# RWKV-7 inside a two-layer trunk: head sums in column blocks of the array, a group norm spread over three steps, and state products pinned next to each other

## The chip, the core and the metric

The kernel runs on one core of a Trainium2 chip. A core has a matrix engine (TensorE, "PE" in the profile, with its weight loads as "PEld"), a vector engine (VectorE, "DVE"), an engine for activations and copies (ScalarE, "ACT"), a general engine (GpSimd, "POOL"), and a sync engine ("SP") that issues most transfers. Each engine works through its own queue in order; they wait for each other through semaphores. The metric is the time of one execution on the device in microseconds (us), the median of several runs.

## The reference

The program is one decoder trunk of two layers on 512 tokens of width 1024, in float32: layer 0 mixes tokens with an RG-LRU block, layer 1 with RWKV-7; each is followed by a gated feed-forward block with a width of 3072. The change touches layer 1's mixer alone:

```python
def _rwkv7_scan(r, w, k, v, aa, bb):
    def step(S, inp):
        r_t, w_t, k_t, v_t, a_t, b_t = inp
        sa = jnp.einsum('bhij,bhj->bhi', S, a_t)
        S = S * w_t[:, :, None, :] + sa[..., None] * b_t[:, :, None, :] + v_t[..., :, None] * k_t[..., None, :]
        y = jnp.einsum('bhij,bhj->bhi', S, r_t)
        return S, y
    ...

def _rwkv7_block(x, ...):
    ...
    r, k, v = rkv[0], rkv[1], rkv[2]
    w = -jax.nn.softplus(-(w0 + jnp.tanh(xw @ w1) @ w2).astype(f32)) - 0.5
    decay = jnp.exp(-jnp.exp(w))
    a = jax.nn.sigmoid((a0 + (xa @ a1) @ a2).astype(f32))
    g = jax.nn.sigmoid(xg @ g1) @ g2
    kk = (kf * k_k).reshape(bsz, seq, RWKV_H, RWKV_N)
    kk = kk / jnp.maximum(jnp.linalg.norm(kk, axis=-1, keepdims=True), 1e-12)
    kf = kf * (1.0 + (a - 1.0) * k_a)
    ...
    y = _rwkv7_scan(rh, hs(decay), kh, vh, -kk, kk * ah)
    mu = jnp.mean(y, axis=-1, keepdims=True)
    var = jnp.mean(jnp.square(y - mu), axis=-1, keepdims=True)
    y = ((y - mu) * lax.rsqrt(var + GN_EPS)).reshape(bsz, seq, d) * ln_w + ln_b
    bonus = jnp.sum(rh * kh * r_k, axis=-1, keepdims=True) * vh
    y = (y + bonus.reshape(bsz, seq, d)).astype(x.dtype)
    return jnp.einsum('btd,de->bte', y * g, w_out)
```

There are 16 heads of 64 channels. Two sums run over the 64 channels of each head: the norm of `kk`, and the bonus. The group norm is over the 64 channels of a head as well.

## The kernel before

**Layout.** Activations lie with channels on the 128 partitions (8 blocks of 128 channels, two heads each) and the 512 tokens along the free dimension. The exact products against large weights are made of three fp32r products, high by high, high by low and low by high (`mm3`, lines 47 to 53); these are the `acc` rows of the profile. Small products with plain float32 operands are recorded as two matmul instructions each. PSUM has 8 banks of 128 x 512 floats, all taken from one pool (`bank`, line 77).

**Who sets the order.** The program is written as a foreground (the large projections) and background tasks, generators that are advanced by a counted number of units between the foreground's products (`push`, `background`, lines 55 to 65; three lanes). From this text a planner makes the order of each engine's queue: it takes what its own timing model believes to be ready, by the order in the text where several are. `tc.keep_in_program_order(ins)` pins an instruction behind the one that the text has just before it on the same engine.

**The decay and the gate `a`** (`second`, inside `rwkv_lora_k`, lines 819 to 851). For each of the 8 blocks two products are made, `l2w` and `l2a`, each a 128-row product followed by a 64-row one into the same bank (lines 840 and 841, 848 and 849). The 64-row product of `l2w` reads partitions 0 to 63, that of `l2a` 64 to 127. They run in the background of the key projection.

**The norm of the keys** (`prepare`, lines 900 to 952). For each half H of the heads (4 blocks) a square `sq` is computed per block and summed over each head by a product with `sel`, a matrix of 8 columns with ones, accumulated over the four blocks into 8 rows of bank `ssq` (line 915). The 8 rows are copied, transposed to tokens (`sst`, line 930), and inverted. It runs behind the key and receptance projections.

**The bonus** (`bonus`, lines 1286 to 1303) has the same form: product `pr` on VectorE, sum over the head by `selk` (8 columns that hold r_k, line 1294) into bank `bon`, copy, transpose (`bont`, line 1300), copy to `bons[H]`.

**The chunk steps** (`rwkv_chunks`, from line 1082). The 512 tokens are 8 chunks of 64. Step n (0 to 16) advances two groups of 4 heads, the second one step behind the first; H=0 takes steps 0 to 8, H=1 steps 8 to 16. A step (`step`, lines 1187 to 1248) issues on TensorE:

- `pe` (line 1200), 8 small products on the state `sv`, copied to `e1`
- the next step's products `s` (`prep_s`), masked by VectorE into `W`
- `between()`, which advances a tail of the group norm, then `fill(0)`: background units
- `pu` and the first part of `py` (lines 1213, 1216), copied to `uv` (line 1220); `prep_t` (transposes `tr`); `fill(1)`
- `pd` (line 1229), from which VectorE makes the next state (lines 1237, 1238, 1240), then the second part of `py` (line 1243), copied to `ytok` (line 1247); `fill(2)`

All heads of a step share one order: for each product the two groups alternate, and the two groups write different column halves of the array.

**The group norm** (`tail`, lines 1250 to 1279), once for every two steps, has three parts. Part one: mean, difference, square (ACT), variance, and a power on POOL (line 1266); also `bv`, the bonus times v, on POOL (line 1263). Part two: three VectorE products (lines 1269 to 1271), the first pinned. Part three: four transposes `pz` on TensorE and four ACT copies into the array that the output projection reads. Part one is issued at the end of an even step, part two in the middle of the next one (`between`), part three at that next step's end.

**The end.** From step 10 the fills are units of `first_half`: four gate products for blocks 0 to 3, then the first half of the output projection (16 units of 6 products). After step 16 come four gate products for H=1, 5.9 units, parts two and three of the last tail, 1.1 units, and the rest (lines 1399 to 1407), then the second half of the output projection. The tag `sq` (three buffers of 128 x 512) is shared by `pr`, `bt`, `ysq`, `bv` and the gate product `yg`.

## Time and profile before

| what | us |
|---|---|
| median of 3 runs (lowest, highest) | 1350.35 (1349.07, 1352.65) |
| the profiled execution | 1353.01 |
| its span, first to last instruction | 1351.3 |

In the profiled execution the layer's stages lie about here: decay, gate and keys 588 to 700 us, the solve of the chunks' triangular systems for H=0 up to 744, steps 0 to 8 from 744 to 838, steps 9 to 16 to 907, the end of the output's first half to 921. A granted clock of 1.00 is TensorE's full speed.

How to read the rows below. A row of the timeline is: start, duration, engine, line, operation, output and inputs, shape, count; in brackets the idle time of the engine before it and what ended it. TensorE's products overlap in their shown durations, so that the distance between two starts is what a product takes. A row of windows is: stretch and its length, then busy time and number of instructions of PE, PEld, DVE, ACT and POOL, the granted clock, the share of the DMA engines, GB/s.

### The profile page before, as it was taken

The numbers are of one execution on the slowest core, as the hardware profiler recorded it, in microseconds if no ns is written. First come the engines' busy times: TensorE is split into PE (matmuls) and PEld (weight loads), VectorE is DVE, ScalarE is ACT, GpSimd is POOL, SyncE is SP. The second block draws the span as 40 slices with busy tenths as digits, with TensorE's granted clock in tenths as the row PEclk, the third lists the DMA queues.
The fourth block names the chain that finished last, engine by engine and source line by source line (L and its number), as shares of the span: only waits on it lengthen the run. The fifth ranks groups of instructions, "written<-read, shape, count | busy, mean of one in ns | idle before, by whom it ended". The sixth has DMA issues, their size and how long they took to land.

```text
span 1351.3 us, 20246 instructions
## 1 busy us (share of the span) xinstructions
PE 1315.4 (97%) x8339; PEld 1062.6 (79%) x8339; DVE 865.4 (64%) x1332; ACT 613.8 (45%) x968; POOL 67.8 (5%) x110
## 2 busy tenths in 40 slices
PE   8999999999999999999999988898999999999998
PEld 7877888888888888866769776676888888888886
DVE  5988756555445756497897977776646464365623
ACT  6797534233233423378635457554634242244311
POOL 4000000000000000020011011120000000000000
PEclk8999999999999999999999889898999999999999
DMA  5423333222323433122222111122323232333311
GB/s 182 121 63 94 100 103 104 84 92 66 108 92 108 128 112 127 56 79 79 63 61 74 56 36 65 56 64 63 113 90 106 66 94 80 109 97 130 115 63 63
DMA packets 72124, 120.27 MB, mean 89 GB/s; under 512 B 9498, under 2 KB 21476, under 8 KB 71904
## 3 DMA queue, kind: packets, MB, share of 16 engines
q1 hardware_dynamic: 70672, 117.20, 27.9%
q8 instruction: 65, 1.06, 0.3%
q10 hardware_dynamic: 576, 1.05, 0.2%
q0 software_dynamic: 784, 0.74, 0.2%
q14 instruction: 27, 0.22, 0.1%
HBM read 114.44 MB, written 4.52 MB: 88 GB/s over the span
## 4 chain that ended last, share of the span: by engine, by line
PE 89%; DVE 5%; ACT 3%; issue 1%; POOL 1%; DMA 1%; SPq 0%; POOLq 0%; ACTq 0%; DVEq 0%
PE acc L51 22%; PE acc L52 22%; PE acc L53 22%; PE acc L616 3%; PE acc L615 3%; PE acc L617 3%; PE acc L986 1%; PE s L1157 1%; PE acc L987 1%; PE acc L988 1%; PE pe L1200 1%; PE ssq L915 1%; PE pd L1229 1%; POOL mu L1266 1%; DMA xin<-in_x_dram 1%
## 5 line engine op out<-in xcount | busy, mean ns | idle before, releaser
L51 PE MATMUL acc<-xs,wh 128*128 128x512 f32 x896 | 352.1, 393 | 0.0
L52 PE MATMUL acc<-xs,wh 128*128 128x512 f32 x896 | 349.9, 390 | 0.0
L53 PE MATMUL acc<-xs,wl 128*128 128x512 f32 x896 | 349.1, 391 | 0.7 <-DVE wl L91 0.7
L91 DVE TENSOR_TENSOR wl<-raw,wh 128x1024 fp32r<-128x1024 f32 (+1 forms) x201 | 242.8, 1216 | 166.3 <-PE acc L52 92.4
L90 ACT CAST wh<-raw 128x1024 fp32r<-128x1024 f32 (+1 forms) x201 | 208.1, 1045 | 259.9 <-DVE wl L91 165.8
L53 PEld LDWEIGHTS acc<-xs,wl 128*128 128x128 f32 x896 | 168.6, 188 | 36.8 <-DVE wl L91 1.2
L51 PEld LDWEIGHTS acc<-xs,wh 128*128 128x128 f32 x896 | 168.8, 188 | 34.8 <-ACT wh L90 0.2
L52 PEld LDWEIGHTS acc<-xs,wh 128*128 128x128 f32 x896 | 168.8, 188 | 34.6 <-issue 0.2
L576 DVE SCALAR_TENSOR_TENSOR cv<-gpad,pv,cv 128x512 f32<-128x512 f32 x96 | 71.9, 749 | 22.2 <-ACT cv L574 21.1
L90 ACT CAST hid<-un 128x512 fp32r<-128x512 f32 x48 | 29.8, 620 | 108.6 <-DVE un L583 108.6
L616 PE MATMUL acc<-wh,hid 128*128 128x512 f32 (+1 forms) x200 | 76.8, 384 | 0.0
L615 PE MATMUL acc<-wh,hid 128*128 128x512 f32 (+1 forms) x200 | 76.5, 383 | 0.0
L617 PE MATMUL acc<-wl,hid 128*128 128x512 f32 (+1 forms) x200 | 75.9, 380 | 0.0
L52 PE MATMUL acc<-hid,wh 128*128 128x512 f32 x192 | 75.7, 394 | 0.0
L53 PE MATMUL acc<-hid,wl 128*128 128x512 f32 x192 | 75.6, 394 | 0.0
L51 PE MATMUL acc<-hid,wh 128*128 128x512 f32 x192 | 75.5, 393 | 0.0
L582 DVE TENSOR_TENSOR un<-acc,rb 128x512 f32<-128x512 f32 x48 | 33.0, 688 | 44.3 <-PE acc L53 44.3
L91 DVE TENSOR_TENSOR hid<-un,hid 128x512 fp32r<-128x512 f32 x48 | 33.2, 691 | 31.4 <-ACT hid L90 31.4
L574 ACT ACTIVATE cv<-gpad,pv 128x512 f32<-128x512 f32 x48 | 39.2, 817 | 20.3 <-DVE gpad L571 20.1
L578 ACT ACTIVATE ge<-cv 128x512 f32<-128x512 f32 x48 | 30.1, 627 | 35.9 <-DVE cv L576 35.9
L620 DVE TENSOR_TENSOR xtok<-xtok,acc 128x512 f32<-128x512 f32 (+1 forms) x25 | 16.7, 666 | 45.2 <-PE acc L617 45.2
L615 PEld LDWEIGHTS acc<-wh,hid 128*128 128x128 f32 x200 | 37.5, 188 | 8.0
(425 smaller groups left out, 2211.9 us busy)
## 6 DMA issues: line engine op xcount, KB each, us to landing
raw<-in_ffn_w_up_dram SPq DMA_DIRECT2D x96, 512.0 KB, 3.9
raw<-in_ffn_w_down_dram SPq DMA_DIRECT2D x48, 512.0 KB, 3.7
raw<-in_rwkv_w_rkv_dram SPq DMA_DIRECT2D x24, 512.0 KB, 3.8
raw<-in_lru_w_in_dram SPq DMA_DIRECT2D x16, 512.0 KB, 3.9
raw<-in_lru_w_out_dram SPq DMA_DIRECT2D x8, 512.0 KB, 3.7
raw<-in_rwkv_w_out_dram SPq DMA_DIRECT2D x8, 512.0 KB, 3.5
xd<-x SPq DMA_DIRECT2D x8, 256.0 KB, 2.0
AR<-xd SPq DMA_DIRECT2D x1, 2048.0 KB, 9.1
```

Of the source, the lines that this page charges most:

```text
L51: nc.tensor.matmul(ps, wh, xh, start=start, stop=False)
L52: nc.tensor.matmul(ps, wh, xl, start=False, stop=False)
L53: nc.tensor.matmul(ps, wl, xh, start=False, stop=stop)
L90: (self.nc.vector.tensor_copy if dve else self.nc.scalar.copy)(hi, src)
L91: self.nc.vector.tensor_tensor(lo, src, hi.bitcast(F32), ALU.subtract)
L574: nc.scalar.activation(cv, gp[:, 0:T], AF.Identity, bias=self.vec(f"ffn_conv_b{l}", fb), scale=cw(0))
L576: nc.vector.scalar_tensor_tensor(cv, gp[:, j : j + T], cw(j), cv, ALU.mult, ALU.add)
L578: nc.scalar.activation(ges[o], cv, AF.Gelu_apprx_tanh)
L582: nc.vector.tensor_tensor(un, ps, rbs[0], ALU.mult)
L615: nc.tensor.matmul(ps, hh[:, s], wh[:, k, m], start=kk == 0, stop=False)
L616: nc.tensor.matmul(ps, hl[:, s], wh[:, k, m], start=False, stop=False)
L617: nc.tensor.matmul(ps, hh[:, s], wl[:, k, m], start=False, stop=kk == 7)
```

## The change

1. **Decay and gate.** Both products of a block get their banks at once: the two 128-row products first, a unit later the two 64-row products next to each other, with row positions 0 and 64.
2. **Head sums.** The sums of `prepare` and `bonus` no longer accumulate over four blocks in 8 rows. Block j writes its own 32 rows of the bank, from a weight of 32 columns at column position 32 j, and the sums are issued in pairs, after the second, and after the fourth block. The copy and the four transposes take all 128 rows; the two useful rows of each 32 are picked out behind them.
3. **Order of the state products.** `pe`, `pd` and the second part of `py` take the two groups in reverse order, and each product is pinned behind the one before it.
4. **Group norm.** `between()` moves from the middle of a step to its end, behind the state's update and `py`; a tail's part two is then issued at the end of the step after part one, part three at the end of the step after that. In step 9 it is called in the middle too, so that both parts run in that step. The first transpose of part three is pinned.
5. **Fills.** Lane 2 gets 1.3, 1.8, 2.0 units per step instead of 1.4, 2.0, 2.1 in the first eight steps; lane 1 gets 0.8 and 1.3 instead of 0.9 and 1.6 from step 8 on. After step 16 part two of the last tail comes first, then the gate products, 3 units, part three, 1 unit.

```diff
@@ second
-                ps = self.bank("l2w")
-                nc.tensor.matmul(ps, ws[0][0][:, s], tw, start=True, stop=False)
-                nc.tensor.matmul(ps, ws[0][1][0:64, s], tw[0:64, :], start=False, stop=True)
+                pw, pa = self.bank("l2w"), self.bank("l2a")
+                nc.tensor.matmul(pw, ws[0][0][:, s], tw, start=True, stop=False)
+                nc.tensor.matmul(pa, ws[1][0][:, s], ta, start=True, stop=False)
+                yield 1
+
+                nc.tensor.matmul(pw, ws[0][1][0:64, s], tw[0:64, :], start=False, stop=True, tile_position=(0, 0))
+                nc.tensor.matmul(pa, ws[1][1][64:128, s], ta[64:128, :], start=False, stop=True, tile_position=(64, 0))
...
@@ prepare
-                nc.tensor.matmul(ssq[0:8, :], sel[:, j, 0:8], sq, start=j == 0, stop=j == 3)
+                sqs.append(sq)
+                for i in (j - 1, j) if j % 2 else ():
+                    nc.tensor.matmul(ssq[32 * i : 32 * i + 32, :], sel[:, 0, 0:32], sqs[i], start=True, stop=True, tile_position=(0, 32 * i))
...
-            ss = t("tmp", 2)[0:8]
-            nc.scalar.copy(ss, ssq[0:8])
+            ss = t("tmp", 2)
+            nc.scalar.copy(ss, ssq)
...
-                nc.tensor.transpose(pt[:, c * 8 : c * 8 + 8], ss[:, c * P : (c + 1) * P], self.ident[0:8, 0:8])
+                nc.tensor.transpose(pt[:, c * P : (c + 1) * P], ss[:, c * P : (c + 1) * P], self.ident)
...
@@ step
+            late = [(i, h, G) for i in range(2) for h in range(2) for G in gs[::-1]]
+            chained = lambda first, ins: ins if first else tc.keep_in_program_order(ins)
...
-            for i, h, (g, bs, H, c, c2, q) in heads:
+            for n_, (i, h, (g, bs, H, c, c2, q)) in enumerate(late):
                 bh = half(1 - q)
-                nc.tensor.matmul(pe[bh, i, h], W[:, h, 2 * g + i, bh], sv[:, 2 * g + i, h], start=True, stop=True, tile_position=(0, 64 - q * 64))
+                chained(n_ == 0, nc.tensor.matmul(pe[bh, i, h], W[:, h, 2 * g + i, bh], sv[:, 2 * g + i, h], start=True, stop=True,
+                                                  tile_position=(0, 64 - q * 64)))
...
-            between()
+            if n == NC + 1:
+
+                between()
             fill(0)
...
+            between()
             fill(2)
@@ tail
-                nc.tensor.transpose(pz[:, i * P : (i + 1) * P], ytok[H, c2][:, i, :], self.ident)
+                put = tc.keep_in_program_order if i == 0 else lambda ins: ins
+                put(nc.tensor.transpose(pz[:, i * P : (i + 1) * P], ytok[H, c2][:, i, :], self.ident))
...
@@ bonus
+                prs.append(pr)
                 yield 1
-                nc.tensor.matmul(pn[0:8, :], selk[:, b, :], pr, start=i == 0, stop=i == 3)
+
+                for j in (i - 1, i) if i % 2 else ():
+                    nc.tensor.matmul(pn[32 * j : 32 * j + 32, :], selk[:, H * 4 + j, :], prs[j], start=True, stop=True, tile_position=(0, 32 * j))
...
@@ the steps' loop
-        self.fills = ((1.2, 1.1, 0.2), (1.0, 0.9, 1.9), (1.4, 2.0, 2.1))
+        self.fills = ((1.2, 1.1, 0.2), (1.0, 0.9, 1.9), (1.3, 1.8, 2.0))
...
+        def trail():
+
+            for t in list(tails):
+                if next(t) == 2:
+                    tails.remove(t)
...
-                self.fills = ((2.9, 0.5, 2.3), (0.9, 0, 1.6), (0, 0, 0))
+                self.fills = ((2.9, 0.5, 2.3), (0.8, 0, 1.3), (0, 0, 0))
...
-            step(n, lambda: [next(t) for t in tails])
+            step(n, trail)
             m = n - 1
             if m > 0 and m % 2:
                 tails.append(tail(m // NC, m % NC // 2))
-                next(tails[0])
-            elif tails:
-                next(tails.pop())
+                next(tails[-1])
...
+        trail()
         gp = [gate_mm(b) for b in range(4, 8)]
-        self.background(5.9, 1)
-        next(tails[0])
-        next(tails.pop())
-        self.background(1.1, 1)
+        self.background(3, 1)
+        trail()
+        self.background(1, 1)
```

`pd` and the second part of `py` change in the same way as `pe`; with a `pd` in the step, the first `py` is pinned behind the last `pd`.

More of the change, by code (lines that the diff above doesn't have):

```diff
@@ L695, in rwkv @@
             PC = big.tile([P, KB, NC], F32, name="PC")
-            selk = big.tile([P, KB, 8], F32, name="selk")
+            selk = big.tile([P, KB, 32], F32, name="selk")
             early = [big.tile([P, 2, 2, T], F32R, tag=f"LT{i}", name=f"early{i}", bufs=1) for i in range(2)]
@@ L838, in second @@
                 s = slice(b * P, (b + 1) * P)
-                ps = self.bank("l2w")
-                nc.tensor.matmul(ps, ws[0][0][:, s], tw, start=True, stop=False)
-                nc.tensor.matmul(ps, ws[0][1][0:64, s], tw[0:64, :], start=False, stop=True)
+                pw, pa = self.bank("l2w"), self.bank("l2a")
[4 more added lines that the diff above has]
+                nc.tensor.matmul(pa, ws[1][1][64:128, s], ta[64:128, :], start=False, stop=True, tile_position=(64, 0))
                 sg = pool.tile([P, T], F32, tag="sg", name="sg", bufs=2)
-                nc.scalar.activation(sg, ps, AF.Sigmoid, bias=self.vec("rwkv_w0", b))
-                yield 1
+                nc.scalar.activation(sg, pw, AF.Sigmoid, bias=self.vec("rwkv_w0", b))
                 for c in range(4):
                     nc.vector.tensor_tensor_scan(AR[b // 4][:, b % 4, c, C : 3 * C], kp, sg[:, c * P : (c + 1) * P], 0.0, ALU.mult, ALU.add)
-                ps = self.bank("l2a")
-                nc.tensor.matmul(ps, ws[1][0][:, s], ta, start=True, stop=False)
-                nc.tensor.matmul(ps, ws[1][1][64:128, s], ta[64:128, :], start=False, stop=True)
-                nc.scalar.activation(self.inner(BK, b), self.bytok(ps), AF.Sigmoid, bias=self.vec("rwkv_a0", b))
+                nc.scalar.activation(self.inner(BK, b), self.bytok(pa), AF.Sigmoid, bias=self.vec("rwkv_a0", b))
                 yield 1
@@ L887, in rwkv_krv @@
             for b in range(KB):
-                c = 2 * (b % 4) + e
-                nc.gpsimd.tensor_copy(selk[hb, b, c : c + 1], self.vec("rwkv_r_k", b)[hb])
+                nc.gpsimd.tensor_copy(selk[hb, b, e : e + 1], self.vec("rwkv_r_k", b)[hb])
         psb = self.bank("back")
@@ L903, in prepare @@
             ssq = self.bank("ssq")
+            sqs = []
             for j in range(4):
@@ L929, in prepare @@
             for c in range(4):
-                nc.tensor.transpose(pt[:, c * 8 : c * 8 + 8], ss[:, c * P : (c + 1) * P], self.ident[0:8, 0:8])
-            pv = pt[:, 0:32].rearrange("p (c h) -> p c h", h=8)
-            nc.vector.tensor_scalar(n8[:, :, 0:8], pv, 1e-24, None, ALU.max)
+                nc.tensor.transpose(pt[:, c * P : (c + 1) * P], ss[:, c * P : (c + 1) * P], self.ident)
+            pv = pt.rearrange("p (c j w) -> p c j w", c=4, w=32)[:, :, :, 0:2]
+            nc.vector.tensor_scalar(n8[:, :, 0:8].rearrange("p c (j e) -> p c j e", e=2), pv, 1e-24, None, ALU.max)
             for part in (32, 0):
@@ L1225, in step @@
                 pd = by_head(self.bank("pd"))
-                for i, h, (g, bs, H, c, c2, q) in heads:
-                    if c < NC - 1:
-                        b = 2 * g + i
-                        nc.tensor.matmul(pd[half(1 - q), i, h], tok[:, b, half(h)], uv[:, b, half(h)], start=True, stop=True, tile_position=(0, 64 - q * 64))
+                live = [x for x in late if x[2][3] < NC - 1]
+                for n_, (i, h, (g, bs, H, c, c2, q)) in enumerate(live):
+                    b = 2 * g + i
+                    chained(n_ == 0, nc.tensor.matmul(pd[half(1 - q), i, h], tok[:, b, half(h)], uv[:, b, half(h)], start=True, stop=True,
+                                                      tile_position=(0, 64 - q * 64)))
                 for g, bs, H, c, c2, q in gs:
@@ L1240, in step @@
                         nc.vector.tensor_tensor(Sn, pd[bh], w[bh], ALU.mult)
-            for i, h, (g, bs, H, c, c2, q) in heads:
+            for n_, (i, h, (g, bs, H, c, c2, q)) in enumerate(late):
                 kh, b = half(q), 2 * g + i
-                nc.tensor.matmul(py[kh, i, h], W[:, h, b, kh], uv[:, b, half(h)], start=False, stop=i + h == 2, tile_position=(0, q * 64))
+                chained(n_ == 0 and not any(c < NC - 1 for _, _, _, c, _, _ in gs),
+                        nc.tensor.matmul(py[kh, i, h], W[:, h, b, kh], uv[:, b, half(h)], start=False, stop=i + h == 2, tile_position=(0, q * 64)))
             for g, bs, H, c, c2, q in gs:
@@ L1278, in tail @@
                 nc.scalar.activation(V[:, c2, b * P : (b + 1) * P], pz[:, i * P : (i + 1) * P], AF.Identity, bias=self.vec("rwkv_ln_b", b))
-            yield 1
+            yield 2
         y = self.x.rearrange("p k t -> p (k t)").rearrange("p (c b t) -> p b c t", c=4, b=KB)
@@ L1288, in bonus @@
             pn = self.bank("bon")
+            prs = []
             for i in range(4):
@@ L1292, in bonus @@
                 nc.vector.tensor_tensor(self.bytok(pr), self.outer(AR, b), self.outer(BK, b), ALU.mult)
+                prs.append(pr)
                 yield 1
-                nc.tensor.matmul(pn[0:8, :], selk[:, b, :], pr, start=i == 0, stop=i == 3)
+                for j in (i - 1, i) if i % 2 else ():
+                    nc.tensor.matmul(pn[32 * j : 32 * j + 32, :], selk[:, H * 4 + j, :], prs[j], start=True, stop=True, tile_position=(0, 32 * j))
             bt = self.xsp.tile([P, T], F32, tag="sq", name="bt", bufs=3)
-            nc.scalar.copy(bt[0:8, :], pn[0:8, :])
+            nc.scalar.copy(bt, pn)
             yield 1
@@ L1299, in bonus @@
             for c in range(4):
-                nc.tensor.transpose(pt[:, c * 8 : c * 8 + 8], bt[0:8, c * P : (c + 1) * P], self.ident[0:8, 0:8])
-            nc.scalar.copy(bons[H], pt[:, 0:32].rearrange("p (c h) -> p c h", h=8))
+                nc.tensor.transpose(pt[:, c * P : (c + 1) * P], bt[:, c * P : (c + 1) * P], self.ident)
+            nc.scalar.copy(bons[H].rearrange("p c (j e) -> p c j e", e=2), pt.rearrange("p (c j w) -> p c j w", c=4, w=32)[:, :, :, 0:2])
             self.done.add(("bonus", H))
```

## The prediction, made before the changed kernel was run

> **What bounds the kernel now.** I read the page first (engine shares, then the chain of work that ended last), then the table of windows over the RWKV stages, then the timeline inside them.

> ```profile
> span 1351.3 us, 20246 instructions
> PE 1315.4 (97%) x8339; PEld 1062.6 (79%) x8339; DVE 865.4 (64%) x1332; ACT 613.8 (45%) x968; POOL 67.8 (5%) x110
> PE 89%; DVE 5%; ACT 3%; issue 1%; POOL 1%; DMA 1%; SPq 0%; POOLq 0%; ACTq 0%; DVEq 0%
> ```

> TensorE is the bound: 97% busy, 89% of the chain. A microsecond of TensorE work saved is worth up to a microsecond, provided no other engine fills the place; where TensorE stands still, only the wait counts. So I need to know, for each edited place, which of the two it is.

> ```profile
> 560.00:626.00 66.00, 66.00 (x274) 46.93 (x272) 51.58 (x97) 44.51 (x67) 12.11 (x36) 1.00 0.24 73
> 626.00:700.00 74.00, 74.00 (x408) 49.12 (x408) 67.12 (x122) 47.18 (x92) 5.75 (x14) 1.00 0.23 68
> ...
> 745.00:755.00 10.00, 10.00 (x179) 7.56 (x177) 9.53 (x24) 4.72 (x12) 0.00 (x0) 1.00 0.18 57
> 755.00:765.00 10.00, 7.67 (x105) 4.95 (x106) 9.47 (x22) 4.27 (x9) 0.00 (x0) 1.00 0.18 42
> ...
> 825.00:835.00 10.00, 9.66 (x220) 6.20 (x220) 8.41 (x17) 7.81 (x22) 3.35 (x3) 1.00 0.01 2
> ...
> 845.00:855.00 10.00, 7.66 (x141) 6.43 (x142) 5.30 (x12) 4.74 (x14) 0.00 (x0) 0.68 0.28 80
> ...
> 915.00:925.00 10.00, 5.18 (x17) 3.72 (x16) 7.11 (x12) 3.55 (x8) 0.00 (x0) 0.73 0.00 1
> ```

> The columns are PE, PEld, DVE, ACT, POOL, then granted clock and DMA. From 560 to 700 us (decay, keys) TensorE never stands still; VectorE has 14 us of air in the first row, 7 in the second. From 745 us (the chunk steps) TensorE has holes, VectorE is nearly full in the first 20 us, and after some holes the clock falls to 0.68 or 0.73.

> **The head sums (`ssq`, `bon`).**

> ```profile
> 625.57 0.39 PE L52 MATMUL acc<-mix,wh 128*128 128x512 f32 x1
> 625.79 0.39 PE L53 MATMUL acc<-mix,wl 128*128 128x512 f32 x1
> 626.11 1.02 PE L915 MATMUL ssq<-tmp,sel 128*8 128x512 f32 x2
> 627.07 0.50 PE L51 MATMUL acc<-mix,wh 128*128 128x512 f32 x1
> 627.40 0.39 PE L52 MATMUL acc<-mix,wh 128*128 128x512 f32 x1
> ...
> 819.73 0.95 PE bon L1294 x2
> ```

> (The last row is of the chain's list.) One sum is two recorded instructions. Neighbouring `acc` products start 0.22 to 0.23 us apart; what counts on TensorE is the distance of starts, since the shown durations overlap. Around the sum the distances are 0.32, 0.96 and 0.33: 0.09 to get in, 0.96 itself, 0.10 to get out, 1.15 us together. There are eight sums in `prepare` and eight in `bonus`, 9.2 us each. After the change two sums with different column blocks stand next to each other. What two neighbours on different columns do is shown by these rows:

> ```profile
> 842.40 0.27 PE L1229 MATMUL pd<-tu 128*64 128x64 f32 x1 [1.91 <-ACT tu L1220]
> ...
> 842.41 0.27 PE L1243 MATMUL py<-tu,W 128*64 128x64 f32 x1
> ```

> `pd` and `py` read all 128 rows and write different column halves: they start 0.01 us apart, though one of them alone is shown with 0.27. A pair of sums should then cost what one does, 1.15 us, and save 1.15. Four pairs in `prepare`: 4.6 us. VectorE has only 7 us of air in those 74, so I take 3.5 (ends 0 and 4.6). In `bonus`, the first half's four sums stand in 745 to 765 us, where VectorE is busy 19.0 of 20: worth nothing there. The second half's begin at 819.73, and from 825 TensorE is busy 9.66 of 10: two pairs, 2.3, of which I take 2 (ends 0 and 4.6). The price is 16 transposes that were of 8 rows and become 128 by 128:

> ```profile
> 833.28 0.41 PE L1300 MATMUL bont<-ident,bt 8*128 8x8 f32 x4
> ...
> 839.84 0.66 PE L1171 MATMUL tr<-ident,BK 128*128 128x128 f32 x4
> ```

> (0.66 - 0.41) / 4 = 0.06 us each, 1.0 us, of which 0.8 on TensorE's path. The copies of 128 instead of 8 partitions keep their 512 columns; the larger memset of `selk` on POOL lies 150 us ahead of its use.

> **The decay and gate products (`l2w`, `l2a`).**

> ```profile
> 601.41 0.50 PE L849 MATMUL l2a<-ta,l2l 64*128 64x512 f32 x1
> ...
> 601.42 0.49 PE L841 MATMUL l2w<-tw,l2l 64*128 64x512 f32 x1
> ...
> 613.36 0.40 PE L848 MATMUL l2a<-ta,l2h 128*128 128x512 f32 x1
> 613.68 0.49 PE L849 MATMUL l2a<-ta,l2l 64*128 64x512 f32 x1
> 614.11 0.50 PE L840 MATMUL l2w<-tw,l2h 128*128 128x512 f32 x1
> ...
> 614.97 0.50 PE L51 MATMUL acc<-mix,wh 128*128 128x512 f32 x1
> ```

> One block's four products take 613.36 to 614.97, 1.61 us, and as behind a sum 0.10 on the next one: 1.71. Once, at 601.41, the two 64-row products happened to be neighbours, and started 0.01 us apart: they use different row halves. With the new order a block is two full products (0.46) and one pair (0.09 in, 613.68 to 614.11 = 0.43, 0.10 out): 1.08. That is 0.63 for seven of eight blocks, 4.4 us; VectorE's 14 us of air cover it, so 4.0 (ends 0, if a pair is torn apart by other work, and 4.6). Two banks are now held instead of one; beside four of `acc` that is six of eight once the `lg` banks are read, so I cost it at nothing; were a ninth wanted, the pair would wait for those reads, at most a block's 1.6 us.

> **The group norm.** Part two of a tail (three VectorE products, the first waiting for POOL's power) stood in the middle of the next step, in front of the state's update; part three, the transposes `pz`, stood in front of the next `pe`.

> ```profile
> 864.60 0.69 DVE L1269 TENSOR_TENSOR ytok<-ytok,mu 128x512 f32<-128x512 f32 x1 [0.57 <-POOL mu L1266]
> ...
> 865.81 0.68 DVE L1270 TENSOR_TENSOR ytok<-ytok,lnw 128x512 f32<-128x512 f32 x1
> 866.53 0.42 DVE L1238 TENSOR_TENSOR sv<-sv,decay 64x256 f32<-64x256 f32 x1
> 866.98 0.69 DVE L1271 TENSOR_TENSOR ytok<-ytok,bv 128x512 f32<-128x512 f32 x1
> 867.82 0.63 PE L1275 MATMUL pz<-ident,ytok 128*128 128x128 f32 x4 [0.91 <-DVE ytok L1271]
> ...
> 869.24 0.68 PE L1200 MATMUL pe<-sv,W 128*64 128x64 f32 x14
> ```

> Three products of 0.69 and a wait of 0.57, 2.6 us, stand before and between the update's instructions (866.53 is one of them), on which `pe` waits until 869.24, and TensorE idles 0.91 for `pz`. Behind the update they run beside the next step's `pe`, `s` and `pu`. I count 2 us here, 1 over the other late steps, and nothing in the first steps, where VectorE is full and the work only moves: 3 (ends 0 and 8). It goes no further because step 9 keeps the middle place:

> ```profile
> 847.26 1.09 PE L1275 MATMUL pz<-ident,ytok 128*128 128x128 f32 x4 [3.43 <-DVE ytok L1271]
> ```

> This 3.43 us hole, and the clock of 0.68 in the window behind it, I expect to see again. The weight row `lnw` that SP loads for the second half waits for that same place, so what queues on SP behind it keeps its time.

> **The end and the fills.**

> ```profile
> 910.43 1.63 POOL L1266 TENSOR_TENSOR mu<-var,mhalf 128x8 f32<-128x8 f32 x1 [11.84 <-DVE var L1265]
> 915.87 0.69 DVE L1353 TENSOR_TENSOR AR<-AR,acc 128x512 f32<-128x512 f32 x1 [2.11 <-PE acc L53]
> 916.48 0.68 DVE L1269 TENSOR_TENSOR ytok<-ytok,mu 128x512 f32<-128x512 f32 x1
> 918.76 0.63 PE L1275 MATMUL pz<-ident,ytok 128*128 128x128 f32 x4 [2.93 <-DVE ytok L1271]
> 921.27 2.07 PE L51 MATMUL acc<-BK,wh 128*128 128x512 f32 x4 [1.89 <-ACT BK L90]
> ```

> The last power is ready at 912.06, but part two sits in VectorE's queue behind the additions of the first projection, the last of which waits for TensorE until 915.87, and starts at 916.48. Now it is issued ahead of them: 4.4 us earlier. What is late next is TensorE itself. Each step from 10 to 16 gives 2.1 units of the output projection instead of 2.5: 7 x 0.4 x 6 products x 0.23 = 3.9 us of fill leave the steps and come to this place, where the idle 2.93 + 1.89 = 4.8 takes them, with 0.9 left. Steps shorter by 3.9, the end by 0.9, and the matmuls from 921.27 to 925 that ran at a clock of 0.73 (3.7 x 0.27 = 1.0): 5.8 (ends 0 and 8).

> Pinning `pe`, `pd`, `py` I cost at nothing: in most steps they already are neighbours, and the pair at 842.40 ran early only to wait.

> **Sum.** -4.0 - 3.5 + 0.8 - 2.0 - 3.0 - 5.8 = -17.5 us. The profiled execution took 1353.01 us (1351.3 of span, 1.7 around it), so 1335.5 for its like; the median, 1350.35, lies 2.7 lower, and 1332.8 is my time.

> **Rivals.** (1) The column blocks don't overlap: the `pd` and `py` rows are 64 columns long, the sums are 512, and nothing in the trace shows two of that length on different columns. Then a pair costs 0.19 + 2 x 0.96 = 2.11 us and saves 0.19 of 2.30: of the 5.5 us counted some 0.9 stay, 1337. [...] The rows at 842.40, two products on all rows, speak against it. (2) The steps are bound by VectorE, so that the moved work takes its place elsewhere: the two tail terms shrink from 8.8 to 2, 1340. For it: 9.5 of 10 busy at 745 and 755. Against: 5.30 at 845. (3) Slower: one buffer of three.

> ```profile
> 858.38 1.36 POOL L1263 TENSOR_TENSOR bv<-x,bon 128x512 f32<-128x512 f32 x1 [14.34 <-DVE BK L91]
> ```

> `bv` takes one of the three buffers tagged `sq`, and POOL already waits for one that the gate products hold. After the change `bv` is held until the end of the next step, and `bonus` holds two. If two gate products can't run in the two buffers left, projection units slip from steps 10 and 11 to the end (2 x 2.1 x 1.4 = 5.9 us with nothing to hide them), the tail terms vanish, and the holes bring the low clock (0.3 of 10 us, in three or four steps, 11): -8.7 + 5.9 + 11 = +8.2, 1358.5. It decides once a third buffer is wanted for a whole step.

> **Chances.** Forecast 0.62 (1320 to 1343), rival 1 0.10, rival 2 0.15 (1336 to 1348), rival 3 0.08, an order that the planner finds better than I see 0.05 (under 1319). A measurement of this kernel can tell about 0.3%, 4 us, from no change: faster than 1346.3 0.84, within 0.08 (the slow ends of rival 2 and of the forecast), slower 0.08. The range, 1319 to 1346, leaves out rival 3 and part of the ends.

> **What would show it.** Two `ssq` and two `bon` rows starting 0.01 us apart, four groups of each; `l2w` and `l2a` 64-row products in eight pairs; no `pz` row with a wait, except step 9's 3.43; the last L1269 within 1 us of POOL's power; the last `acc` wait on BK under 1 us. The prediction is wrong if pairs are torn apart, if 626 to 700 us keeps its length with VectorE full, or if the steps wait for buffers.

## The result, and the profile after

The changed kernel takes 1328.8 us (median of four, 1326.38 to 1330.94), the kernel before 1350.49 beside it: ratio 0.9827, 95% interval 0.9813 to 0.9842. The profiled execution took 1328.46 us.

The page of the changed kernel, the lines that answer to the three quoted first of before:

```profile
span 1326.7 us, 20245 instructions
PE 1295.2 (98%) x8339; PEld 1055.3 (80%) x8339; DVE 860.3 (65%) x1332; ACT 614.0 (46%) x968; POOL 67.9 (5%) x110
PE 88%; DVE 6%; ACT 3%; issue 1%; DMA 1%; POOL 0%; SPq 0%; POOLq 0%; DVEq 0%; ACTq 0%
```

TensorE is still the bound, with as many instructions as before, and POOL's share of the chain falls from 1% to 0%. To see where the time went, cut the span where the same instruction stands in both kernels: the first `l2` product, the first `pe` of steps 0, 9 and 16. Identical code in front of the first `l2` product differs by up to 4.1 us between profiled executions (590.1 us in e3, 594.3 in e11), so lengths are compared and not points in time. The windows of the last three stages, before and then after (length, PE busy, ..., granted clock):

```profile
744.46:837.69 93.23, 84.04 (x1605) 68.55 (x1604) 75.00 (x151) 54.93 (x129) 12.36 (x11) 0.91 0.13 37
837.69:902.66 64.97, 55.16 (x989) 43.02 (x989) 51.21 (x94) 38.36 (x93) 11.05 (x8) 0.95 0.25 83
902.66:1351.29 448.63, 437.52 (x1978) 360.86 (x1978) 237.73 (x309) 153.28 (x207) 6.53 (x7) 0.99 0.29 91
```

```profile
740.06:823.00 82.94, 73.96 (x1606) 64.00 (x1605) 72.56 (x151) 54.09 (x126) 11.61 (x11) 0.96 0.15 42
823.00:881.20 58.20, 49.08 (x968) 38.15 (x967) 46.44 (x89) 37.34 (x94) 10.96 (x8) 0.94 0.25 82
881.20:1326.68 445.48, 439.20 (x2001) 362.86 (x2000) 241.23 (x314) 155.47 (x209) 6.52 (x7) 1.00 0.30 93
```

| stage | before | after | measured | forecast |
|---|---|---|---|---|
| first `l2` product to first `pe` | 150.8 | 146.7 | -4.1 | -6.7 |
| steps 0 to 8 | 93.2 | 82.9 | -10.3 | -2.0 |
| steps 9 to 15 | 65.0 | 58.2 | -6.8 | -6.9 |
| from step 16 on | 448.6 | 445.5 | -3.1 | -1.9 |

The forecast's 0.8 for the transposes stands in the first stage. The total hides misses in both directions: the first stage gave less, steps 0 to 8 five times as much. Of the 20.2 us behind the first `pe`, TensorE idle less (length less PE busy, summed over three windows: 30.1 before, 24.4 after) is 5.7. The largest part shows in windows around the low clock, of before and of after:

```profile
766.00:773.00 7.00, 7.00 (x95) 6.29 (x88) 6.09 (x14) 2.66 (x8) 1.18 (x1) 0.51 0.02 6
786.50:793.50 7.00, 6.03 (x106) 5.47 (x106) 1.35 (x4) 3.00 (x9) 0.00 (x0) 0.51 0.01 2
813.50:817.50 4.00, 4.00 (x96) 3.38 (x96) 3.35 (x5) 3.07 (x7) 0.00 (x0) 0.57 0.01 4
844.50:851.50 7.00, 4.24 (x88) 3.83 (x92) 3.61 (x9) 2.38 (x8) 0.00 (x0) 0.51 0.39 115
919.50:926.50 7.00, 5.22 (x12) 4.13 (x13) 4.98 (x8) 3.54 (x8) 0.00 (x0) 0.51 0.01 4
```

```profile
758.50:762.50 4.00, 4.00 (x76) 3.71 (x75) 3.84 (x10) 1.34 (x4) 1.04 (x1) 0.57 0.41 131
779.00:783.00 4.00, 3.94 (x98) 3.79 (x99) 2.31 (x5) 1.68 (x3) 1.25 (x2) 0.57 0.01 4
830.00:837.50 7.50, 5.82 (x75) 4.63 (x75) 4.28 (x9) 2.26 (x7) 0.00 (x0) 0.54 0.38 107
```

Length times (1 - clock) is the most that a window loses: 3.4, 3.4, 1.7, 3.4 and 3.4 us before, 1.7, 1.7 and 3.4 after. It comes in portions of 1.7 us, 3.4 us at half clock: nine before, four after, 8.5 us less. TensorE also stands still in some of these windows (busy 4.24 and 5.22 of 7.00), and that time is in the idle time already; with PE's busy time in place of the length, the loss is 12.7 us before and 6.1 after, 6.6 less. With 6.6 + 5.7, four pairs of `bon` at 1.15 less eight larger transposes at 0.06 (4.1), 3.8 us of the 20.2 are left; the pinned products give 2.7 of that in steps 0 to 8 (e6, below), and the rest is open.

These are two single executions. That of before took 1353.01 us, 2.5 above its median, at a mean granted clock of 0.986. Over all executions the median of this clock is 0.988 before and 0.992 after; (1 - clock) times the span is 16.2 and 10.6 us. Of the 21.7 us between the two median times the clock's part is thus at most 5.6.

The pairs. One timeline of the changed kernel, head sums of `prepare` and of `bonus`:

```profile
627.75 0.39 PE L53 MATMUL acc<-mix,wl 128*128 128x512 f32 x1
628.07 1.05 PE L918 MATMUL ssq<-tmp,sel 128*32 128x512 f32 x4
629.05 0.50 PE L51 MATMUL acc<-mix,wh 128*128 128x512 f32 x1
...
811.08 1.05 PE L1311 MATMUL bon<-pr,selk 128*32 128x512 f32 x4
```

Four instructions, two sums, last 1.05 us, where one sum's two lasted 1.02: the column blocks run beside each other. All four `bon` pairs and three of four `ssq` pairs came out so. Of the eight `l2` blocks only four kept their pair; the first block here is whole, the second torn:

```profile
607.85 0.39 PE L840 MATMUL l2w<-tw,l2h 128*128 128x512 f32 x1
608.08 0.40 PE L841 MATMUL l2a<-ta,l2h 128*128 128x512 f32 x1
608.41 0.49 PE L844 MATMUL l2w<-tw,l2l 64*128 64x512 f32 x1
608.41 0.50 PE L845 MATMUL l2a<-ta,l2l 64*128 64x512 f32 x1
608.84 0.50 PE L840 MATMUL l2w<-tw,l2h 128*128 128x512 f32 x1
```

```profile
603.26 0.40 PE L840 MATMUL l2w<-tw,l2h 128*128 128x512 f32 x1
603.58 0.50 PE L844 MATMUL l2w<-tw,l2l 64*128 64x512 f32 x1
604.01 0.50 PE L841 MATMUL l2a<-ta,l2h 128*128 128x512 f32 x1
604.44 0.50 PE L845 MATMUL l2a<-ta,l2l 64*128 64x512 f32 x1
604.87 0.50 PE L52 MATMUL acc<-mix,wh 128*128 128x512 f32 x1
```

The whole block takes 0.99 us, the torn one 1.61 as before: the planner put both products on `l2w` first. In step 9, and at the end (timeline; idle time and its releaser in brackets):

```profile
831.68 1.12 PE L1288 MATMUL pz<-ident,ytok 128*128 128x128 f32 x4 [2.94 <-DVE ytok L1283]
...
890.23 1.63 POOL L1278 TENSOR_TENSOR mu<-var,mhalf 128x8 f32<-128x8 f32 x1 [9.46 <-DVE var L1277]
891.90 0.69 DVE L1281 TENSOR_TENSOR ytok<-ytok,mu 128x512 f32<-128x512 f32 x1 [1.81 <-POOL mu L1278]
894.55 0.60 PE L1288 MATMUL pz<-ident,ytok 128*128 128x128 f32 x4
894.91 0.48 PE L51 MATMUL acc<-BK,wh 128*128 128x512 f32 x1
```

Part two follows its power at once (890.23 + 1.63 = 891.86) and no product waits behind it: 2.93 and 1.89 us of idle are gone. Step 9 keeps its hole, and the half clock at 830 begins in it.

### The profile page after: what moved, and what is told of

Its sections match the earlier page's. It is cut to its first block, busy times and chain, and to the rows that moved or that the text cites. A ratio compares the mean times of both kernels' runs of the same rounds, so it can differ in the third digit from the quotient of the medians.

```text
span 1326.7 us, 20245 instructions
## 1 busy us (share of the span) xinstructions
PE 1295.2 (98%) x8339; PEld 1055.3 (80%) x8339; DVE 860.3 (65%) x1332; ACT 614.0 (46%) x968; POOL 67.9 (5%) x110
## 3 DMA queue, kind: packets, MB, share of 16 engines
q10 hardware_dynamic: 576, 1.05, 0.2%
## 4 chain that ended last, share of the span: by engine, by line
PE 88%; DVE 6%; ACT 3%; issue 1%; DMA 1%; POOL 0%; SPq 0%; POOLq 0%; DVEq 0%; ACTq 0%
PE acc L51 22%; PE acc L53 22%; PE acc L52 22%; PE acc L616 3%; PE acc L615 3%; PE acc L617 3%; PE s L1160 1%; PE acc L989 1%; PE acc L990 1%; PE acc L991 1%; PE pe L1206 1%; DVE W L1167 1%; DMA xin<-in_x_dram 1%; DVE X L1043 1%; DVE sv L1248 1%
## 5 line engine op out<-in xcount | busy, mean ns | idle before, releaser
L51 PE MATMUL acc<-xs,wh 128*128 128x512 f32 x896 | 352.0, 393 | 0.0
L53 PE MATMUL acc<-xs,wl 128*128 128x512 f32 x896 | 348.9, 390 | 0.7 <-DVE wl L91 0.7
L52 PE MATMUL acc<-xs,wh 128*128 128x512 f32 x896 | 349.6, 390 | 0.0
L91 DVE TENSOR_TENSOR wl<-raw,wh 128x1024 fp32r<-128x1024 f32 (+1 forms) x201 | 242.9, 1216 | 163.4 <-PE acc L52 95.0
L90 ACT CAST wh<-raw 128x1024 fp32r<-128x1024 f32 (+1 forms) x201 | 207.9, 1045 | 257.7 <-DVE wl L91 169.6
L53 PEld LDWEIGHTS acc<-xs,wl 128*128 128x128 f32 x896 | 168.5, 188 | 36.8 <-DVE wl L91 1.2
L51 PEld LDWEIGHTS acc<-xs,wh 128*128 128x128 f32 x896 | 168.8, 188 | 35.0 <-ACT wh L90 0.2
L52 PEld LDWEIGHTS acc<-xs,wh 128*128 128x128 f32 x896 | 168.7, 188 | 34.5 <-DVE wl L91 0.2
L90 ACT CAST hid<-un 128x512 fp32r<-128x512 f32 x48 | 29.8, 620 | 108.7 <-DVE un L583 108.7
L52 PE MATMUL acc<-hid,wh 128*128 128x512 f32 x192 | 75.7, 394 | 0.0
L53 PE MATMUL acc<-hid,wl 128*128 128x512 f32 x192 | 75.6, 394 | 0.0
L51 PE MATMUL acc<-hid,wh 128*128 128x512 f32 x192 | 75.5, 393 | 0.0
L91 DVE TENSOR_TENSOR hid<-un,hid 128x512 fp32r<-128x512 f32 x48 | 33.2, 691 | 31.5 <-ACT hid L90 31.5
L578 ACT ACTIVATE ge<-cv 128x512 f32<-128x512 f32 x48 | 30.1, 627 | 35.6 <-DVE cv L576 35.6
```

The costliest lines, as they stand in the source:

```text
L51: nc.tensor.matmul(ps, wh, xh, start=start, stop=False)
L52: nc.tensor.matmul(ps, wh, xl, start=False, stop=False)
L53: nc.tensor.matmul(ps, wl, xh, start=False, stop=stop)
L90: (self.nc.vector.tensor_copy if dve else self.nc.scalar.copy)(hi, src)
L91: self.nc.vector.tensor_tensor(lo, src, hi.bitcast(F32), ALU.subtract)
L578: nc.scalar.activation(ges[o], cv, AF.Gelu_apprx_tanh)
```

## The experiments

All times are medians. The stages are those above, of each run's one profiled execution, which can lie some us off the median (1353.01 us for before, 1325.82 for e7, 1320.69 for e12); "half clock" is the most that the low-clock windows between the first `pe` and 30 us behind that of step 16 lose, in us.

| run | time | ratio to before, interval | first stage | steps 0-8 | steps 9-15 | from 16 | half clock |
|---|---|---|---|---|---|---|---|
| before | 1350.5 | | 150.8 | 93.2 | 65.0 | 448.6 | 15.4 |
| e1 `l2` alone | 1349.80 | 0.9992 (0.9982-1.0002) | 148.9 | 92.2 | 64.9 | 448.6 | 13.7 |
| e2 sums alone | 1350.38 | 0.9996 (0.9986-1.0006) | 146.8 | 93.6 | 66.8 | 448.1 | 18.8 |
| e3 norm alone | 1339.54 | 0.9915 (0.9900-0.9930) | 150.8 | 88.1 | 62.9 | 445.5 | 8.5 |
| e4 pins alone | 1349.03 | 0.9985 (0.9975-0.9995) | 150.8 | 90.7 | 64.6 | 448.0 | 13.7 |
| **after** | 1328.80 | 0.9827 (0.9813-0.9842) | 146.7 | 82.9 | 58.2 | 445.5 | 6.8 |
| e5 no `bonus` sums | 1336.63 | 0.9893 (0.9877-0.9910) | 146.7 | 92.0 | 57.2 | 445.5 | 6.8 |
| e6 no pins | 1332.62 | 0.9855 (0.9841-0.9870) | 146.7 | 85.6 | 58.5 | 445.6 | 6.8 |
| e7 no fills | 1330.69 | 0.9838 (0.9816-0.9860) | 146.7 | 84.1 | 58.9 | 443.8 | 6.8 |
| e8 pairs pinned | 1327.90 | 0.9828 (0.9812-0.9845) | 147.1 | 83.0 | 58.1 | 445.5 | 6.8 |
| e9 no norm, no fills | 1344.55 | 0.9950 (0.9933-0.9966) | 146.6 | 89.8 | 64.9 | 448.6 | 13.6 |
| e10 norm and sums | 1334.44 | 0.9876 (0.9861-0.9891) | 146.8 | 87.0 | 60.0 | 445.3 | 6.8 |
| e11 `l2` pinned | 1327.35 | 0.9819 (0.9802-0.9836) | 144.1 | 82.5 | 59.5 | 445.5 | 8.5 |
| e12 step 9 too | 1323.85 | 0.9797 (0.9784-0.9810) | 144.1 | 81.5 | 52.6 | 448.4 | 1.7 |

**One part at a time.** To the kernel before, only the new order in `second`:

```diff
+                nc.tensor.matmul(pw, ws[0][0][:, s], tw, start=True, stop=False)
+                nc.tensor.matmul(pa, ws[1][0][:, s], ta, start=True, stop=False)
+                yield 1
+                nc.tensor.matmul(pw, ws[0][1][0:64, s], tw[0:64, :], ..., tile_position=(0, 0))
+                nc.tensor.matmul(pa, ws[1][1][64:128, s], ta[64:128, :], ..., tile_position=(64, 0))
```

> The kernel before with the new order of l2w and l2a alone. In the trace of the changed kernel only four of the eight pairs of 64-row products start together; the planner put the others in the order of the block. If that is why the forecast 4.0 us became about 1.8, then here again some four pairs form and the time from the first l2w product to the first pe is 1.5 to 2.5 us shorter than before, the total 1348 to 1349. If instead VectorE took the gain back later (its stretch 626 to 700 us is nearly full), the last l2w product comes 1.8 us earlier but the first pe at its old place, the total 1350.

The first stage is 1.9 us shorter: before had one pair by chance, four stand here, and 3 x 0.63 = 1.9. The time itself is not told from no change.

Only the sums in column blocks, in `prepare` and `bonus`:

```diff
+                for i in (j - 1, j) if j % 2 else ():
+                    nc.tensor.matmul(ssq[32 * i : 32 * i + 32, :], sel[:, 0, 0:32], sqs[i], ..., tile_position=(0, 32 * i))
...
+                for j in (i - 1, i) if i % 2 else ():
+                    nc.tensor.matmul(pn[32 * j : 32 * j + 32, :], selk[:, H * 4 + j, :], prs[j], ..., tile_position=(0, 32 * j))
```

> The kernel before with the head sums in column blocks alone (keys' norm and bonus). By the price from the rows, 1.15 us a pair: seven or eight pairs, less 0.8 for the transposes. Theory 1 (as in the prediction: VectorE is full in the first steps, the first two bonus pairs are worth nothing): steps 0 to 8 shorter by 2, the first pe earlier by 2.5 to 3.5, total about 1345. Theory 2 (TensorE's order counts there too): steps 0 to 8 shorter by 4 to 5, total 1342 to 1343.

Neither expected time came. The first stage gains 4.0 us and steps 0 to 2 gain 3.8 (together 26.7 for 30.5; 1.7 of it is a portion of half clock less), and by the medians all of it is given back. The second half's `bon` waits, here in step 7 (timeline of e2):

```profile
822.32 0.69 DVE L1272 TENSOR_TENSOR ytok<-ytok,mu 128x512 f32<-128x512 f32 x1 [1.43 <-POOL mu L1269]
822.92 0.68 DVE L1296 TENSOR_TENSOR pr<-AR,BK 128x512 f32<-128x512 f32 x1
823.66 1.91 PE L1301 MATMUL bon<-pr,selk 128*32 128x512 f32 x2 [2.67 <-DVE pr L1296]
```

`pr` stands behind part two of the norm, which waits 1.43 us for POOL; TensorE idles 2.67, then runs at half clock: the row holds one sum's two products, 1.91 us for 1.02, and the pair is torn. Step 7 takes 13.2 us for 9.3. Half clock costs 3.4 us more than before.

Only the norm's new places, in the steps and at the end, with its first `pz` pinned, without the fills:

```diff
-            between()
+            if n == NC + 1:
+                between()
...
+            between()
             fill(2)
```

> The kernel before with the group norm's parts moved and the new order at the end, without new fills and without the pins of pe, pd and py. Theory 1 (as in the prediction): steps 0 to 8 the same within 1 us, steps 9 to 15 shorter by 2 to 3, the end (start of step 16 to the first product of the second half) shorter by 3 to 5, total 1343 to 1345. Theory 3 (the tail held up the first steps too, in which most of the unforeseen 7 us were gained): steps 0 to 8 shorter by 5 or more, total 1337 to 1340.

This is the largest single part, 11 us. In steps 0 to 8 it takes 5.1 us away, and TensorE idles no less there (10.2 us for 9.2); half clock in these steps falls from 8.5 to 1.7. The holes became smaller and more numerous, and fewer are followed by a slow spell.

Only the pinned `pe`, `pd`, `py`:

```diff
+                chained(n_ == 0, nc.tensor.matmul(pe[bh, i, h], ...
```

> The kernel before with pe, pd and py in reversed, pinned order alone. Theory 1 (they were neighbours already): the same within 1.5 us, 1349 to 1352. Theory 4 (the order of the planner changes with them, and the unforeseen gain in steps 0 to 8 is theirs): steps 0 to 8 shorter by 4 or more, total under 1346.

2.2 us less than the kernel before beside it (1351.22). In steps 0 to 8, 1.7 us is one portion of half clock; of the rest, length less idle less half clock falls from 75.5 to 73.7. Which products take less was not shown.

**One part taken out of the changed kernel.** The sums of `bonus` as before (8 columns, accumulated in one block):

```diff
-                for j in (i - 1, i) if i % 2 else ():
-                    nc.tensor.matmul(pn[32 * j : 32 * j + 32, :], ...)
+                nc.tensor.matmul(pn[0:8, :], selk[:, b, :], pr, start=i == 0, stop=i == 3)
```

> The changed kernel with the old bonus sums (8 columns, one after the other), all else as changed. Alone, the sums gained 3.8 us in steps 0 to 2 and lost 5.2 in steps 3 and 7, where a sum stood in TensorE's queue and its product on VectorE behind part two of a tail, which waits for POOL's power. Theory A (that wait is gone with the tail's move, so the sums keep their gain): steps 0 to 8 longer than in the changed kernel by 3 to 4.6, total 1332 to 1333.5. Theory B (VectorE's fullness bounds steps 0 to 2, and the sums gain nothing): within 1 us, total 1328 to 1330.

7.8 us slower, steps 0 to 8 9.1 us longer, twice what was expected; of that, 2.8 in steps 0 to 2, where the forecast gave the first half's sums nothing. Step 6 takes 19.9 us for 10.0, partly since 23 `acc` products stand in it that stand in steps 3 to 5 of the changed kernel; steps 3 to 6 together are 5.6 us longer, 3.4 of them half clock (timeline and window of e5):

```profile
804.72 0.94 PE L1066 MATMUL m1p<-XN,O 32*32 32x32 f32 x25 [2.23 <-DVE XN L1049]
```

```profile
805.00:816.00 11.00, 11.00 (x176) 10.16 (x173) 6.31 (x13) 5.41 (x12) 1.80 (x3) 0.54 0.01 3
```

A wait of 2.23 us (1.51 at the same place of the changed kernel) is followed by three portions of half clock, 5.1 us.

The pins left out (the loops over `heads` again), then the fills set back:

```diff
-            for n_, (i, h, (g, bs, H, c, c2, q)) in enumerate(late):
+            for i, h, (g, bs, H, c, c2, q) in heads:
```

> The changed kernel with pe, pd and py in the old order and without their pins. Theory A (the planner's old order already had them as neighbours, and the 2.5 us that the pins alone gained in steps 0 to 8 came from the tail's products, which they kept away from the state's): total within 1.5 us of the changed kernel, 1327 to 1330. Theory B (the pins have a gain of their own): steps 0 to 8 longer by 2.5 or more, total 1331 to 1333.

```diff
-        self.fills = ((1.2, 1.1, 0.2), (1.0, 0.9, 1.9), (1.3, 1.8, 2.0))
+        self.fills = ((1.2, 1.1, 0.2), (1.0, 0.9, 1.9), (1.4, 2.0, 2.1))
...
-                self.fills = ((2.9, 0.5, 2.3), (0.8, 0, 1.3), (0, 0, 0))
+                self.fills = ((2.9, 0.5, 2.3), (0.9, 0, 1.6), (0, 0, 0))
```

> The changed kernel with the old numbers of background units in the steps. The parts taken alone add up to 0.8 us in steps 9 to 15 and 1.7 at the end, the whole change brought 6.8 and 4.9. Theory A (the difference is the fills: 0.4 units a step less, 3.9 us, which fill the end's holes): steps 9 to 15 longer by 4 or more, the end the same or shorter, total 1332 to 1336. Theory B (the parts need each other, the fills little): steps 9 to 15 longer by under 2, total 1328 to 1331.

The pins are worth 3.8 us in this kernel (the intervals just touch), 2.7 of them in steps 0 to 8, where idle time (8.9 us for 9.0) and half clock stay as they were. A gain of the fills is not shown: 1.9 us by the medians, with overlapping intervals, while the stages add up to 733.5 us and 733.3. With the old fills 66 instead of 48 products of the output projection stand in steps 9 to 15 (18 x 0.23 = 4.1 us of work), and those steps are 0.7 us longer, not 4: they fill holes. Also, the last `bon` pair is torn with the old fills and waits for `pr`, 1.2 us here and 1.1 in e10 below.

The torn pairs, first try: `pa`'s 64-row product pinned behind the one ahead of it, and the `ssq` pair issued in the other order with its second sum pinned:

```diff
-                for i in (j - 1, j) if j % 2 else ():
+                for i in (j, j - 1) if j % 2 else ():
+                    put = self.tc.keep_in_program_order if i % 2 == 0 else lambda ins: ins
...
+                self.tc.keep_in_program_order(nc.tensor.matmul(pa, ws[1][1][64:128, s], ...))
```

> The changed kernel with the second 64-row product of each block pinned behind the first, and the second sum of each key norm's pair pinned behind the other. In the changed kernel four of eight and three of four pairs formed. If the torn pairs are the whole of what the decay and gate products lacked (forecast 4.0, measured about 1.9), the time from the first l2w product to the first pe is shorter by 2.5 (four pairs by 0.63) to 3.5 (and one by 1.15), total 1325 to 1326.5. If what is saved there waits for VectorE or for the inverse of the norm later, it stays within 1 us, 1328 to 1330.

All four `ssq` pairs are whole, still four of eight `l2` pairs: a pin keeps an order, and the planner put `pa`'s full product in between. The stage is not shorter. Its window behind the wait for `rec` is at half clock here (e8), and is not in the changed kernel (after, with the wait):

```profile
649.00:653.00 4.00, 4.00 (x26) 2.72 (x25) 4.00 (x5) 2.08 (x4) 0.00 (x0) 0.57 0.16 59
```

```profile
648.82 1.19 PE L950 MATMUL knb<-rec,back 40*128 40x512 f32 x4 [1.17 <-DVE rec L944]
...
648.82:653.00 4.18, 4.18 (x31) 2.94 (x32) 4.15 (x6) 3.68 (x7) 0.00 (x0) 1.00 0.57 194
```

That costs 1.7 us, against the 1.15 of the mended pair.

**What makes the gain together.** The changed kernel with the norm in its old place and the old fills; the kernel before with the moved norm and the sums alone:

> The changed kernel with part two and part three of the group norm back in their old places, and with the old fills (pairs, column blocks and pinned products stay). Theory (the sums gain in the steps only because the norm's part two no longer stands in front of the products `pr` on VectorE): the two waits of `bon` for `pr` that the sums alone showed, 4.2 us and 2.7 us, come back in steps 3 and 7; steps 0 to 8 take 90 to 93 us, steps 9 to 15 64 to 67, and the first stage keeps its 146.7: 1344 to 1349 us. Rival (the pinned products are enough to let the sums gain): steps 0 to 8 take 85 to 87 us, 1337 to 1341.

> The kernel before with the moved group norm and the sums in column blocks alone: no `l2` pairs, no pinned products, old fills. Theory (these two together carry the gain, by four pairs of `bon` of 1.15 us and by fewer spells of low clock): steps 0 to 8 take 83 to 86 us, as in the changed kernel without the pins (85.6), steps 9 to 15 take 59 to 63, and the time is 1330 to 1335 us. Rival (the pins or the fills are needed as well): steps 0 to 8 stay at the 88.1 that the moved norm showed alone, and the time is 1336 to 1340.

Without the norm's move (e9) the sums, pairs and pins together save 6 us. The wait for `pr` is back in step 7 (timeline of e9), behind the norm's first product as in e2; in step 3 a wait of 3.67 stands too, but it is for a weight `wh` of ScalarE, not for `pr`, as the 4.2 us of e2 were, so this half of the expectation fell:

```profile
820.12 0.69 DVE L1278 TENSOR_TENSOR ytok<-ytok,mu 128x512 f32<-128x512 f32 x1 [1.42 <-POOL mu L1275]
820.73 0.68 DVE L1302 TENSOR_TENSOR pr<-AR,BK 128x512 f32<-128x512 f32 x1
821.47 1.05 PE L1307 MATMUL bon<-pr,selk 128*32 128x512 f32 x2 [1.65 <-DVE pr L1302]
```

With the norm and the sums alone (e10) 16 of the 21.7 us are there; steps 0 to 8 stay a microsecond above what was expected. Sums that are worth nothing alone (e2) are worth 5 on top of the moved norm (1339.5 to 1334.4). The last column sorts the runs: every kernel with the norm in its old place loses 13.6 us or more to half clock, every one with the new place 8.5 or less. The other executions agree: over all of a kernel's the median of the mean granted clock is 0.983 to 0.988 with the old place, 0.991 to 0.994 with the new.

**Two further steps.** To the changed kernel three pins in each block, for the `l2` pairs:

```diff
+                self.tc.keep_in_program_order(nc.tensor.matmul(pa, ws[1][0][:, s], ta, ...))
                 yield 1
+                self.tc.keep_in_program_order(nc.tensor.matmul(pw, ws[0][1][0:64, s], ...))
+                self.tc.keep_in_program_order(nc.tensor.matmul(pa, ws[1][1][64:128, s], ...))
```

> The changed kernel with three of a block's four `l2` products pinned behind one another (both full ones, then both of 64 rows), so that all eight pairs of 64-row products stand next to each other instead of four. Theory (a torn pair costs what the forecast said, 1.71 - 1.08 = 0.63 us, and TensorE is the bound of that stage): four more pairs, 2.5 us out of the 146.7 of the first stage, 1326.3 us. Rival (a later wait, such as the 1.17 us for `rec`, takes it, as it did for the pinned `ssq` pairs): the first stage keeps 146 to 147 us and the time stays within 1 us of the changed kernel.

Seven pairs are whole instead of four, 3 x 0.63 = 1.9 us, and the wait for `rec` falls from 1.17 to 0.46: the first stage is 2.6 us shorter. The profile has one portion of half clock more in step 12, and the time, 1.45 less, can't be told from that of the changed kernel.

And step 9 like the others, on top of it:

```diff
-            if n == NC + 1:
-                between()
...
-            if n == NC + 1:
+            if n == NC + 2:
                 load_lnw(1)
...
-            if n == NC + 1:
+            if n == NC + 2:
                 self.push(first_half(), 1)
```

> The kernel with the pinned `l2` products, and step 9 treated as the other steps: parts two and three of the norm behind the update there too, the load of `lnw` for the second half issued ahead of step 10 instead of step 9, and the first half's output projection begun one step later. Theory (the hole of step 9 and the low clock behind it are the price of the middle place): the idle 2.94 us in front of `pz` goes, `pe` of step 10 starts 2 to 3 us earlier, the 1.2 us that the low clock takes in step 9 go too, and the two units of projection that step 10 loses (2 x 6 x 0.23 = 2.8 us) only move to the end: steps 9 to 15 take 52 to 55 us and the end 447 to 449, 1322 to 1325 us. Rival (step 10 without fills only gets the hole that step 9 had): steps 9 to 15 shorten by no more than the end grows, 1326 to 1329.

1323.85 us, faster than both kernels. The last two windows and the start of step 10 (e12):

```profile
817.67:870.26 52.59, 44.01 (x955) 34.40 (x955) 45.48 (x88) 37.18 (x94) 11.30 (x8) 1.00 0.25 86
870.26:1318.62 448.36, 442.07 (x2013) 365.15 (x2012) 242.12 (x315) 155.73 (x209) 6.84 (x8) 1.00 0.29 93
```

```profile
823.93 0.33 PE L1206 MATMUL pe<-sv,W 128*64 128x64 f32 x2 [0.51 <-DVE sv L1247]
825.01 0.68 PE L1206 MATMUL pe<-sv,W 128*64 128x64 f32 x14 [0.38 <-DVE sv L1245]
```

`pe` of step 10 begins 6.3 us behind that of step 9 (9.7 after), waits for the state alone, and steps 9 to 15 have no low clock in this execution. It is the fastest of five, at a mean clock of 0.997; the others, at 0.992 to 0.995, lost more. The end is 2.9 us longer, for 12 products more (2.8).

## Why the prediction held, and which of its steps did not

- **TensorE is the bound; column blocks overlap.** Right. Rival 1 gave a pair 2.11 us, the changes at its two ends included; by the starts in the rows it takes 0.98, with the same 0.19 around it 1.17. Both sums use all 128 rows, and in a later `ssq` pair of the changed kernel (both sums begin at 672.87 us) two weight loads start at 672.90, 0.03 us behind the start of both products; the second products of both sums start at 673.32.
- **Head sums of `prepare`, -3.5.** Right: -4.0 alone (e2).
- **`l2`, -4.0.** The price of a pair was right (0.63; e11), the count wrong: seven new pairs were forecast, three came. The end of the range, "a pair is torn apart by other work", was what happened. In the stage as a whole 0.9 more goes to `rec` (1.17 us of wait for 0.30 in e2), and a torn `ssq` pair.
- **`bonus`, first half "worth nothing there".** This step failed. The quoted row of 745 to 755 showed VectorE at 9.53 of 10, but TensorE at 10.00 of 10, and it was TensorE's work that counted: steps 0 to 2 are 2.8 us longer without the pairs (e5). Where the four sums stand in the kernel before, 748.24 to 760.75 us, TensorE never idles:

```profile
748.00:761.00 13.00, 13.00 (x189) 8.63 (x187) 12.33 (x30) 5.78 (x14) 0.00 (x0) 1.00 0.13 42
```

- **Group norm, -3.0, "nothing in the first steps, where VectorE is full and the work only moves".** This step failed most. The norm alone gives 11 us, 5.1 in steps 0 to 8. It was right that the idle time there would not shrink (9.2 to 10.2 in e3). What was missed is the clock behind the holes: the forecast used the low clock once, at 921 us, and expected the rest to stay. In e3's profile nine portions became five by this part alone.
- **Step 9's hole, expected again.** Right: 2.94 for 3.43, with two portions of half clock behind it. e12 shows what it cost.
- **End and fills, -5.8.** The end was right in mechanism, and larger: both waits are gone, 4.8 us, and 3.4 us of half clock, 2.6 of them under products, went where 1.0 was taken; with 4.1 us of moved products that is -3.3, and -3.1 was measured from step 16 on. The 3.9 us that the steps were to lose with their fills are not there (0.7 in e7): the fills had stood in holes. That steps 9 to 15 met their sum (-6.8 for -6.9) is luck: norm, sums and pins gave what the fills did not; e9 (64.9) and e10 (60.0) put most of it on the norm with the sums.
- **Pins at nothing.** Wrong: 2.2 us alone, 3.8 in the changed kernel. How they save it stays open.
- **Rivals 2 and 3.** The steps did get shorter, so VectorE did not take the moved work's place; no `bon` or `pz` of steps 0 to 8 waits in the changed kernel, and with the old fills (e7) as many products of the projection stand in steps 9 to 15 as before, 66, so none slipped for want of a third `sq` buffer.
- **The total.** It came inside the range with terms wrong in both directions (`l2` and fills too large, `bonus`, norm and pins too small), so the nearness of -17.5 to -21.7 is in part luck.

Why the norm's new place makes fewer holes end in half clock: every pair of runs shows that it does, and the traces point to the size of the holes. The spells lie on a grid of 3.413 us (last section). Laid at every possible offset over the steps and the 30 us behind the start of step 16, such a grid has on average 6.2 cells in which TensorE is busy under 47% in the kernel before, 3.9 in e3, 2.5 in the changed kernel and 1.5 in e12. This is worked out from the traces, not tested by a run of its own.

## What to carry to other kernels

Where TensorE stands at 10 of 10 in a window, count its work there at full price, however busy another engine is: here, with VectorE at 12.33 of 13.00, two pairs priced at 1.15 us each were worth 2.8 (e5). Beside the idle time of each hole, add up TensorE's busy time times (1 - granted clock) in the windows behind it: here that fell by 6.6 us, as large as any other term, and in steps 0 to 8 half clock fell from 8.5 to 1.7 with a change that did not shorten the idle time there (9.2 to 10.2, e3). A pin that keeps an order doesn't keep two products adjacent (e8: four of eight `l2` pairs), so count the pairs in the trace before pricing them all.

## What the runs showed of the hardware

```profile
779.06 0.76 PE L1206 MATMUL pe<-sv,W 128*64 128x64 f32 x10 [2.95 <-DVE sv L1248]
...
775.75:779.16 3.41, 0.46 (x7) 0.29 (x7) 3.30 (x8) 1.92 (x2) 0.94 (x1) 1.00 0.23 79
779.16:782.57 3.41, 3.41 (x92) 3.29 (x95) 2.15 (x5) 1.41 (x2) 0.90 (x1) 0.50 0.02 5
```

```profile
775.49 0.63 PE L1206 MATMUL pe<-sv,W 128*64 128x64 f32 x14 [2.96 <-DVE sv L1245]
...
770.82:774.24 3.42, 1.71 (x15) 1.51 (x13) 3.38 (x5) 3.22 (x5) 0.02 (x1) 1.00 0.46 153
774.24:777.65 3.41, 2.16 (x97) 2.06 (x97) 3.28 (x8) 1.41 (x2) 0.92 (x1) 1.00 0.02 5
```

So of two equal holes the one that lay within a cell of the grid was followed by half clock, and the one split between two cells was not. No cell had to be idle throughout: cells in which TensorE was busy for half their length and more were followed by half clock too (before: 66% from 810.42 us on). What decides between 47 and 71% was not shown. Where the grid lies differs from trace to trace (766.05 us before, 758.68 after and 753.77 in e12 are 1.46, 0.92 and 2.84 us past a multiple of 3.41333), so the count of portions in one profile is in part luck, and a part whose gain is less than a portion, 1.7 us, can be hidden by one, as the mended `ssq` pair was in e8.
